# Seven-product units of the feed-forward layers: weight blocks of 256 features, and two up units of each convolved layer as seven products

## Chip, core and metric

The kernel runs on one core of one Trainium2 chip. The metric is the device time of one execution in microseconds, taken as the median of the executions shown. Lower is better.

## What is computed

Two transformer blocks act on one sequence of 512 tokens of 1024 features, in float32. Each of three layers ends in a feed-forward layer; those three are what the change is about (cut from the reference):

```python
gu = n2 @ w_ffn_in[l]                                    # first block, 1024 -> 2 x 2816
ff = (jax.nn.silu(gu[..., :D_FF]) * gu[..., D_FF:]) @ w_ffn_out[l]
...
u = h @ w_up                                             # second block, twice
for j in range(FFN_CONV):
    y = y + u_pad[:, j:j + S, :] * conv_w[j]             # 3 taps over the tokens, and a bias
gate, up = jnp.split(y, 2, axis=-1)
return (jax.nn.silu(gate) * up) @ w_down
```

The first block's layer is called layer 1 here; the second block has two, with a convolution over the tokens after the up projection: layers 2 and 3. The rest (pooling, stick-breaking attention, cross attention, a gated recurrence and latent attention) is not touched.

## The kernel before, in words

Every float32 product is made of three matmuls. `split` (L62 on ScalarE, ACT; L65 on VectorE, DVE) turns a float32 operand into two parts, `hi` (a rounded copy, by ACT) and `lo` (the remainder, source minus `hi`, by DVE). `mm3` then issues hi·hi, hi·lo and lo·hi into one PSUM bank (L108, L109, L110). Weights come by DMA on the SP queue into `raw` tiles and are split into tiles of tag `w`, a ring of 8, which is room for the parts of four blocks. A part can be written only when TensorE (PE) has done with the block four places earlier.

`out_proj`, `ffn` and the helpers are a plain program; a scheduler then fixes the order of the instructions on each engine, and each engine works its own list off in that order, waiting at the head of the list where it must.

`ffn` works through the 2816 = 22 x 128 gate features and as many up features. For f = 0 the program comes from the layer before (`projA_first`). After that the loop takes 256 gate and 256 up features at a time, f = 2, 4, ... 20. There are two ways to make such a piece:

- `projA`, the straight way: 2 feature blocks x 8 rows of 128 inputs x 3 matmuls over all 512 tokens, 48 matmuls of 512 columns. Its weights are two `raw` loads, each split as one 128x1024 tile.
- `seven`: the weights are cut in a 2 x 2 grid (feature block i, input half j), the tokens in two halves, and seven products of sums take the place of eight. A product is here 4 x 3 = 12 matmuls of 256 columns. The sums of weights (`usum`, tiles `u` and `raw`) are made by DVE, the sums of the input once in `x_sums` (tiles `xc`). Three PSUM accumulators X, Y, Z hold the results; ACT copies Y out, and DVE adds the copies to X and Z.

In layer 1 both gate and up pieces go by `seven` (`gate7`, `up7`), interleaved: `tail` carries the last products of an up unit into the next gate unit. In layers 2 and 3 gate pieces go by `seven`, up pieces by `projA`. There `mixed` follows: one ACT instruction and two DVE instructions (L68, tile `y`) for each 128 features, then `Silu` on ACT or a multiplication into `FT` on DVE. Since DVE's list is in order, a part that stands behind an instruction that waits is late with it.

In layer 1 the loop also draws `rotation`, a chain of some 45 small DVE instructions for the sine tables of the last attention.

Of the kernel before, what the change touches and what calls it, by code (L numbers as in the profile page):

```python
# [10 lines left out]
F32 = mybir.dt.float32  # L11
# [23 lines left out]
def kernel(ctx: ExitStack, tc: tile.TileContext, a: dict, out: bass.AP):  # L35
# [13 lines left out]
    sp = ctx.enter_context(pool("sp", bufs=6))  # L49
# [254 lines left out]
    def seven(w, col, ops, xp, dst, c21, done):  # L304

        A = []
        for i in range(2):
            raw = (wp, xp)[i].tile([P, KD, P], F32, tag="raw", name=nm("raw"), bufs=2)  # L310
            load(raw, w[:, col + i * P : col + (i + 1) * P].rearrange("(k p) n -> p k n", p=P))
            A.append([raw.rearrange("p (c j) n -> p j c n", j=2)[:, j] for j in range(2)])
        bY, bXZ = bank("Y"), bank("XZ")
        pY, pX, pZ = bY[:, :256], bXZ[:, :256], bXZ[:, 256:]
# [9 lines left out]
        def usum(a_, b_, o=None):  # L324
            if o is None:
                o = xp.tile([P, 4, P], F32, tag="u", name=nm("u"), bufs=2)
            tt(o, a_, b_, ALU.add)
            return o

        product(pY, A[0][0], (0, 0), True)  # L330
        act(dst[0][:, lf], pY, AF.Copy)
        yield 1
        u1 = usum(A[1][0], A[1][1])
        product(pX, u1, "nT1", True)
        u3 = usum(A[0][0], A[1][0], A[1][0])
# [70 lines left out]
    negC_f = row("negC_f")[:, :P]  # L406
    load(negC_f, a["c_neg_causal"])
    identR = cp.tile([P, P], F32R, name="identR")
    act(identR, ident, AF.Copy)
    negS = cp.tile([P, P], F32R, name="negS")  # L410
    act(negS, negS_f, AF.Copy)
    negC = cp.tile([P, P], F32R, name="negC")
    act(negC, negC_f, AF.Copy)
# [139 lines left out]
    def rotation(E):  # L553

        pos_i = E.tile([P, NT], I32, name="pos_i")
        load(pos_i, a["positions_2"][0].rearrange("(t p) -> p t", p=P))
        pos = E.tile([P, NT], F32, name="pos")
        nc.vector.tensor_copy(pos, pos_i)
        frq = E.tile([P, 32], F32, name="frq")
        load(frq, a["c_freq"].unsqueeze(0).to_broadcast([P, 32]))  # L560

        ang, part, tmp = (E.tile([P, NT, 32], F32, name=nm("rot")) for _ in range(3))
        prod, turn, frac = ang, sinT, cosT
        tt(ang, pos.unsqueeze(2).to_broadcast([P, NT, 32]), frq.unsqueeze(1).to_broadcast([P, NT, 32]), ALU.mult)
# [23 lines left out]
        for n_, c in enumerate(pieces):  # L588
            add_turns(angh.bitcast(F32), c, n_ == 0)
# [189 lines left out]
    def out_proj(w, Y, nk, gpost, gnext, half0, nxt, plain=lambda: None, parts=None):  # L779
# [74 lines left out]
        else:  # L854
# [633 lines left out]
```

## Time and profile before

| | us |
|---|---|
| median of 3 runs | 2029.02 (2028.67 to 2031.72) |
| the profiled execution | 2036.45, its span 2034.6 |
| PE busy / DVE busy / ACT busy | 1990.5 / 1277.1 / 958.0 |
| layer 1, first unit to first matmul of the down projection | 198.0 |
| layer 2, the same with the idle time ahead of it | 211.9 |
| layer 3, the same | 213.1 |

PE is the engine that is busy nearly all the time, so the time is read from PE: how many matmuls it issues, at which spacing, and where it waits. A matmul's own duration is longer than the spacing, because matmuls overlap; the spacing is the difference of two starts. The same is true of DVE: two instructions in a row start closer than the duration of one. The granted TensorE clock is 0.993 of full speed over the span.

### The profile page before, as it was taken

To read this page: it belongs to the slowest core of one execution; us is meant where nothing else is said; L and a number is where in the kernel's file an instruction comes from. 1 tells how busy PE (TensorE), PEld (TensorE's weight loads), DVE (VectorE), ACT (ScalarE), POOL (GpSimd) and SP (SyncE) were. 2 spreads that over 40 slices of the span, in tenths; PEclk is the share of its full clock that TensorE was granted. 3 is DMA by queue.
4 is the path that set the end of the run, shared out by engine and by line. 5 is a ranking of instruction groups with operands and counts; after the bars stand their busy time and mean duration, and the time that the engine had idled before them with its cause. 6 is when DMAs were issued, how large, how long until landed. Compare 5 with 4: busy or idle time off the path is not lost.

```text
span 2034.6 us, 29719 instructions
## 1 busy us (share of the span) xinstructions
PE 1990.5 (98%) x11665; PEld 1701.7 (84%) x11665; DVE 1277.1 (63%) x2293; ACT 958.0 (47%) x1862; POOL 56.4 (3%) x84
## 2 busy tenths in 40 slices
PE   8999999999999999999999999999989999999999
PEld 6877778889999888888888888888887778888887
DVE  5664543489888336666556887853555558887632
ACT  5543452365555227333244555542357545555521
POOL 0000000000000000000010000000021000000000
PEclk9999999999999999999999999999989999999999
DMA  6332224324333332222213233332230113333322
GB/s 223 90 92 73 69 77 124 104 84 125 102 106 105 93 93 84 73 63 72 70 46 89 83 113 96 93 105 93 66 96 32 42 48 106 96 104 94 104 93 83
DMA packets 192482, 183.44 MB, mean 90 GB/s; under 512 B 6999, under 2 KB 159830, under 8 KB 192342
## 3 DMA queue, kind: packets, MB, share of 16 engines
q1 hardware_dynamic: 192342, 181.54, 29.6%
q8 instruction: 92, 1.51, 0.3%
q14 instruction: 48, 0.39, 0.1%
HBM read 179.42 MB, written 2.10 MB: 89 GB/s over the span
## 4 chain that ended last, share of the span: by engine, by line
PE 80%; DVE 9%; DMA 5%; ACT 3%; issue 2%; POOL 1%; SPq 0%; DVEq 0%; POOLq 0%; ACTq 0%
PE B L108 10%; PE B L110 10%; PE B L109 10%; PE A L108 9%; PE A L109 9%; PE A L110 8%; PE hs L1099 2%; DVE wu L65 2%; PE Y L108 2%; PE Y L109 2%; PE Y L110 2%; DMA raw<-in_w_ffn_in_dram 2%; PE XZ L108 2%; PE XZ L109 2%; PE XZ L110 2%
## 5 line engine op out<-in xcount | busy, mean ns | idle before, releaser
L65 DVE TENSOR_TENSOR wlo<-raw,whi 128x1024 fp32r<-128x1024 f32 (+2 forms) x217 | 257.2, 1187 | 343.7 <-ACT whi L62 343.3
L62 ACT ACTIVATE whi<-raw 128x1024 fp32r<-128x1024 f32 (+2 forms) x217 | 223.9, 1033 | 376.5 <-PE B L109 256.5
L108 PE MATMUL A<-XH,whi 128*128 128x512 f32 (+1 forms) x912 | 337.1, 370 | 0.2 <-ACT XH L62 0.2
L109 PE MATMUL A<-XL,whi 128*128 128x512 f32 (+1 forms) x912 | 332.4, 365 | 0.8 <-DVE XL L65 0.8
L110 PE MATMUL A<-XH,wlo 128*128 128x512 f32 (+1 forms) x912 | 331.7, 364 | 0.0
L110 PE MATMUL B<-whi,yc 128*128 128x512 f32 x528 | 208.0, 395 | 0.0
L108 PE MATMUL B<-whi,yc 128*128 128x512 f32 x528 | 207.6, 393 | 0.0
L109 PE MATMUL B<-wlo,yc 128*128 128x512 f32 x528 | 207.3, 393 | 0.0
L110 PEld LDWEIGHTS A<-XH,wlo 128*128 128x128 f32 x912 | 173.1, 190 | 29.5 <-issue 0.2
L109 PEld LDWEIGHTS A<-XL,whi 128*128 128x128 f32 x912 | 173.3, 190 | 26.4 <-DVE XL L65 1.2
L108 PEld LDWEIGHTS A<-XH,whi 128*128 128x128 f32 x912 | 172.8, 190 | 26.8 <-ACT XH L62 0.7
L108 PE MATMUL B<-whi,XH 128*128 128x512 f32 (+2 forms) x416 | 166.8, 402 | 1.3 <-ACT whi L62 1.3
L109 PE MATMUL B<-wlo,XH 128*128 128x512 f32 (+2 forms) x416 | 158.7, 382 | 1.0 <-DVE wlo L65 1.0
L110 PE MATMUL B<-whi,XL 128*128 128x512 f32 (+2 forms) x416 | 158.7, 383 | 0.0
L108 PE MATMUL Y<-xc,wu 128*128 128x256 f32 x480 | 133.8, 279 | 5.0 <-ACT g L62 3.2
L110 PE MATMUL Y<-xc,wu 128*128 128x256 f32 x480 | 133.0, 277 | 0.0
L109 PE MATMUL Y<-xc,wu 128*128 128x256 f32 x480 | 132.9, 277 | 0.0
L62 ACT ACTIVATE wu<-raw 128x512 fp32r<-128x512 f32 x160 | 98.8, 624 | 46.2 <-DMA raw<-in_ffn_w_up_dram 34.9
L62 ACT ACTIVATE wu<-u 128x512 fp32r<-128x512 f32 x120 | 74.4, 629 | 96.8 <-PE A L109 59.8
L109 PEld LDWEIGHTS B<-wlo,yc 128*128 128x128 f32 x528 | 99.3, 188 | 22.7
L110 PEld LDWEIGHTS B<-whi,yc 128*128 128x128 f32 x528 | 99.4, 188 | 21.8
L108 PEld LDWEIGHTS B<-whi,yc 128*128 128x128 f32 x528 | 99.4, 188 | 21.8 <-issue 0.4
(325 smaller groups left out, 4201.0 us busy)
## 6 DMA issues: line engine op xcount, KB each, us to landing
raw<-in_ffn_w_up_dram SPq DMA_DIRECT2D x88, 512.0 KB
raw<-in_w_ffn_in_dram SPq DMA_DIRECT2D x44, 512.0 KB
raw<-in_ffn_w_down_dram SPq DMA_DIRECT2D x44, 512.0 KB
raw<-in_w_in_dram SPq DMA_DIRECT2D x42, 512.0 KB
raw<-in_hgrn_w_in_dram SPq DMA_DIRECT2D x32, 512.0 KB
raw<-in_w_ffn_out_dram SPq DMA_DIRECT2D x22, 512.0 KB
raw<-in_w_out_dram SPq DMA_DIRECT2D x8, 512.0 KB
raw<-in_hgrn_w_out_dram SPq DMA_DIRECT2D x8, 512.0 KB
```

The source lines that it names most:

```text
L62: return nc.scalar.activation(out=out_, in_=in_, func=func, **kw)
L65: return nc.vector.tensor_tensor(out=out_, in0=in0, in1=in1, op=op)
L108: nc.tensor.matmul(out_, lhsT=sta[0], rhs=mov[0], start=first, stop=False, **kw)
L109: nc.tensor.matmul(out_, lhsT=sta[0], rhs=mov[1], start=False, stop=False, **kw)
L110: nc.tensor.matmul(out_, lhsT=sta[1], rhs=mov[0], start=False, stop=last, **kw)
L1099: nc.tensor.matmul(b[:, sl], lhsT=K[:, e, sl], rhs=Q[:, e, sl], start=True, stop=True)
```

## The change

- `seven` now takes blocks of 256 features: a unit covers 512 gate or up features, a product is 24 matmuls of 256 columns into a whole bank (two feature blocks q side by side), a sum or a part is one 128x1024 tile. The weights of a unit are four loads of 128x4x256 in place of two of 128x8x128. The first, (0, 0), goes into the `raw` tiles of the ring pool, the other three into three `raw` tiles of the layer's own pool, which gate and up units share one after the other. There is one `u` tile. Y alternates between the banks c0 and c1, Z between c2 and c3, X is one of the four common banks.
- the loop takes f = 2, 6, 10, 14, 18. In layer 1 all five up units go by `seven` as before; in layers 2 and 3 those of f = 6 and 10 do now, the others stay two `projA`. The new up units keep partial results in `FT` rows 18 to 21.
- `rotation` is drawn by the down projection of layer 1, in one scratch tile; `negC` is loaded ahead of the latent attention; the small tiles' pool `sp` has 5 buffers in place of 6.

```diff
-    def seven(w, col, ops, xp, dst, c21, done):
+    def seven(w, col, ops, xp, place, quarter):
...
+        for i, j in ((0, 0), (1, 0), (1, 1), (0, 1)):
+            if (i, j) == (0, 0):
+                t_ = wp.tile([P, 4, 256], F32, tag="raw", name=nm("raw"), bufs=2)
+            else:
+                t_ = xp.tile([P, 4, 256], F32, tag="raw", name=nm("raw"), bufs=3)
+            src = w[:, col + i * 256 : col + (i + 1) * 256].rearrange("(c j p) n -> p j c n", j=2, p=P)[:, j]
+            load(t_, src)
+            blk[i, j] = t_
+        n_ = uz[0] = uz[0] + 1
+        bY, bX, bZ = bank("Y", f"c{n_ % 2}"), bank("X"), bank("Z", f"c{2 + n_ % 2}")
...
         def product(o, src, key, first):
-            t_ = wp.tile([P, 2, 4, P], F32R, tag="w", name=nm("wu"))
-            split(src, t_[:, 0], t_[:, 1])
+            hi = wp.tile([P, 4, 256], F32R, tag="w", name=nm("wuh"))
+            lo = wp.tile([P, 4, 256], F32R, tag="w", name=nm("wul"))
+            split(src, hi, lo)
             x_ = ops[key]
-            for c in range(4):
-                mm3(o, (t_[:, 0, c], t_[:, 1, c]), (x_[0][:, c], x_[1][:, c]), first and c == 0, c == 3, skip_group_check=True)
+            for q in range(2):
+                f_ = slice(q * P, (q + 1) * P)
+                for c in range(4):
+                    mm3(
+                        o[:, q], (hi[:, c, f_], lo[:, c, f_]), (x_[0][:, c], x_[1][:, c]),
+                        first and q == 0 and c == 0, q == 1 and c == 3, skip_group_check=True,
+                    )
...
+        product(pY, blk[0, 0], (0, 0), True)
+        a_ = kept(pY, 0, 0)
         yield 1
+        u1 = usum(blk[1, 0], blk[1, 1], xp.tile([P, 4, 256], F32, tag="u", name=nm("u")))
         product(pX, u1, "nT1", True)
+        u3 = usum(blk[0, 0], blk[1, 0], blk[1, 0])
+        u2 = usum(u3, blk[1, 1], u1)
         product(pY, u2, "nT2", False)
+        b_ = kept(pY, 0, 1)
+        product(pZ, blk[0, 1], (1, 0), True)
+        quarter(0, 0, pZ, 1.0, a_)
         product(pY, u3, "T3", False)
+        c_ = kept(pY, 1, 1)
+        quarter(1, 1, pX, -1.0, c_)
         yield 1
+        product(pY, blk[1, 1], "T4", False)
+        quarter(1, 0, pY, -1.0, None)
+        product(pX, usum(u2, blk[0, 1], u2), (1, 1), False)
+        quarter(0, 1, pX, 1.0, b_)
...
-            for f in range(0, 22, 2):
-                next(rot, 0)
...
+            for f in range(2, 22, 4):
                 g7 = gate7(f)
                 next(g7)
                 run(tail)
                 next(g7)
-                if conv is None:
+                tail = iter(())
+                if f in ups:
                     tail = up7(f)
                     next(tail)
                     run(g7)
...
                     run(g7)
                     run(u8)
+                    run(projA(w_up, DFF + (f + 2) * P, X, sink(up, f + 2)))
             run(tail)
-            r = out_proj(w_down, FT, 22, gpost(), gnext(), lambda g0: xpool, nxt, parts=E)
+            rot = rotation(E) if conv is None else iter(())
+            r = out_proj(w_down, FT, 22, gpost(), gnext(), lambda g0: xpool, nxt, parts=E, beside=rot)
```

**How the order moves.** In the rows below `wuh` and `wul` are the parts hi and lo of a product's weights, `u` a sum of weights, `raw` a loaded block or a sum made in its place, `X`, `Y`, `Z` the accumulators, `y` the convolution's tile. The numbers tell one tile from another.

DVE in layer 2 with the change, from the sixth product's part of the gate unit of f = 6 to the first sums of the up unit of f = 6:

```order
L65 TENSOR_TENSOR wul_1737_10728<-raw_1711_10531,wuh_1736_10727 128x1024 [waits PE_49,Activation_49]
L65 TENSOR_TENSOR FT_1575_9600<-Z_1715_10537,FT_1575_9600 128x2x256 [waits PE_49]
L65 TENSOR_TENSOR wul_1741_10768<-u_1718_10567,wuh_1740_10767 128x1024 [waits Activation_49]
L65 TENSOR_TENSOR u_1744_10806<-raw_1728_10689,raw_1729_10691 128x1024 [waits DMAHW7_49,DMAHW0_49,DVE_49]
L65 TENSOR_TENSOR raw_1728_10689<-raw_1727_10687,raw_1728_10689 128x1024 [waits DVE_49]
```

and the loads of that up unit on the SP queue:

```order
L77 DMA raw_1728_10689<-in_ffn_w_up_2_dram 128x4x256 [waits DMAHW2_49,DMAHW7_49,DVE_49,Activation_49]
L77 DMA raw_1729_10691<-in_ffn_w_up_2_dram 128x4x256 [waits DVE_49]
L77 DMA raw_1730_10693<-in_ffn_w_up_2_dram 128x4x256 [waits DMAHW1_49,DVE_49]
```

`raw_1729` takes the place of `raw_1711`, so its load waits for the first DVE row above; the fourth row waits for that load. Two instructions stand between. Before, a unit's second block had one of two tiles, and the loads of one unit did not wait for the unit just before it.

DVE in layer 2 with the change, from the gate unit's last drain of f = 10 into the up unit of f = 10:

```order
L68 SCALAR_TENSOR_TENSOR y_1790_11234<-FT_1575_9600,convc_334,y_1790_11234 128x510 [waits DVE_49]
L68 SCALAR_TENSOR_TENSOR y_1791_11239<-FT_1575_9600,convc_334,y_1791_11239 128x510 [waits DVE_49]
L65 TENSOR_TENSOR FT_1575_9600<-X_1758_10935,FT_1575_9600 128x2x256 [waits PE_49]
L65 TENSOR_TENSOR wul_1798_11287<-u_1796_11284,wuh_1797_11286 128x1024 [waits Activation_49]
L68 SCALAR_TENSOR_TENSOR y_1794_11274<-FT_1575_9600,convc_334,y_1794_11274 128x511 [waits Activation_49]
L68 SCALAR_TENSOR_TENSOR y_1795_11279<-FT_1575_9600,convc_334,y_1795_11279 128x511 [waits Activation_49]
L68 SCALAR_TENSOR_TENSOR y_1794_11274<-FT_1575_9600,convc_334,y_1794_11274 128x510 [waits DVE_49]
L68 SCALAR_TENSOR_TENSOR y_1795_11279<-FT_1575_9600,convc_334,y_1795_11279 128x510 [waits DVE_49]
L65 TENSOR_TENSOR u_1796_11284<-raw_1780_11167,raw_1781_11169 128x1024
L65 TENSOR_TENSOR wul_1800_11317<-u_1796_11284,wuh_1799_11316 128x1024 [waits Activation_49]
L65 TENSOR_TENSOR wul_1802_11346<-raw_1782_11171,wuh_1801_11345 128x1024 [waits DMAHW1_49,Activation_49]
L65 TENSOR_TENSOR wul_1804_11375<-raw_1780_11167,wuh_1803_11374 128x1024 [waits Activation_49]
```

DVE at that place before, where the up piece is a `projA`:

```order
L65 TENSOR_TENSOR wlo_1837_11389<-raw_1835_11386,whi_1836_11388 128x1024 [waits DMAHW5_49,PE_49]
L68 SCALAR_TENSOR_TENSOR y_1819_11286<-A_1807_11177,convc_338,y_1819_11286 128x511 [waits Activation_49]
L65 TENSOR_TENSOR wu_1838_11416<-raw_1823_11295,wu_1838_11416 128x512 [waits PE_49,Activation_49]
L68 SCALAR_TENSOR_TENSOR y_1819_11286<-A_1807_11177,convc_338,y_1819_11286 128x510 [waits DVE_49]
L65 TENSOR_TENSOR wu_1840_11438<-u_1829_11333,wu_1840_11438 128x512 [waits PE_49,Activation_49]
L65 TENSOR_TENSOR FT_1624_9915<-FT_1624_9915,y_1819_11286 128x512 [waits DVE_49]
L65 TENSOR_TENSOR wlo_1844_11462<-raw_1842_11459,whi_1843_11461 128x1024 [waits DMAHW6_49,PE_49,Activation_49]
L65 TENSOR_TENSOR g7_1820_11291<-XZ_1825_11298,g7_1820_11291 128x256 [waits PE_49]
```

With the change the parts of the up unit's second and third products (`wul_1798`, `wul_1800`) stand behind the gate unit's last drain of X and behind four and eight `y` instructions; before, the parts of the gate unit's products 6 and 7 (`wu`) and of the straight piece (`wlo`) stood between single `y` instructions.

PE at that place with the change, where the gate unit's last product ends and the up unit's second begins:

```order
L108 MATMUL X_1758_10935<-XH_1576_9601,wuh_1792_11245 128x256
L109 MATMUL X_1758_10935<-XL_1577_9602,wuh_1792_11245 128x256
L110 MATMUL X_1758_10935<-XH_1576_9601,wul_1793_11246 128x256
L108 MATMUL X_1784_11174<-xc_1651_10009,wuh_1797_11286 128x256 [waits Activation_49]
L109 MATMUL X_1784_11174<-xc_1652_10010,wuh_1797_11286 128x256
L110 MATMUL X_1784_11174<-xc_1651_10009,wul_1798_11287 128x256 [waits DVE_49]
```

The product that needs `wul_1798` follows at once on the one whose accumulator DVE drains in the row ahead of `wul_1798`; before, a straight piece of 24 matmuls of 512 columns stood there.

## Rows read from the trace of the kernel before

**Rows 1.** The page: span, and busy time of each engine.

```profile
span 2034.6 us, 29719 instructions
...
PE 1990.5 (98%) x11665; PEld 1701.7 (84%) x11665; DVE 1277.1 (63%) x2293; ACT 958.0 (47%) x1862; POOL 56.4 (3%) x84
```

**Rows 2.** Busy time by stretch: layer 1, its down projection, layer 2, one of its periods, layer 3.

```profile
core 0: us, PE busy (x) PEld busy (x) DVE busy (x) ACT busy (x) POOL busy (x), PEclk, DMA share, GB/s
453.49:651.47 197.98, 192.14 (x1659) 189.80 (x1657) 175.95 (x336) 115.45 (x233) 0.00 (x0) 1.00 0.36 105
651.47:772.00 120.53, 120.21 (x538) 98.81 (x537) 44.28 (x51) 37.52 (x51) 2.20 (x4) 1.00 0.30 92
1126.63:1338.48 211.85, 208.39 (x1323) 186.02 (x1321) 179.49 (x269) 121.79 (x199) 0.00 (x0) 1.00 0.35 102
1226.56:1268.00 41.44, 41.44 (x266) 37.11 (x264) 34.49 (x52) 23.07 (x39) 0.00 (x0) 1.00 0.36 103
1696.28:1909.34 213.06, 209.35 (x1323) 187.38 (x1321) 179.21 (x268) 123.86 (x199) 0.00 (x0) 0.99 0.34 102
```

**Rows 3.** Timeline of PE in layer 2: start, duration, instruction. Two products, then half a straight piece.

```profile
1185.12 0.28 PE L108 MATMUL Y<-xc,wu 128*128 128x256 f32 x1
...
1187.73 0.28 PE L110 MATMUL XZ<-XH,wu 128*128 128x256 f32 x1
1187.84 0.39 PE L108 MATMUL A<-XH,whi 128*128 128x512 f32 x1
...
1193.20 0.40 PE L110 MATMUL A<-XH,wlo 128*128 128x512 f32 x1
1193.44 0.28 PE L108 MATMUL Y<-XH,wu 128*128 128x256 f32 x1
```

**Rows 4.** Timeline of PE in layer 1; in brackets the idle time ahead and what ended it.

```profile
453.49 0.28 PE L108 MATMUL Y<-XH,wu 128*128 128x256 f32 x1
...
524.77 0.39 PE L108 MATMUL XZ<-XH,wu 128*128 128x256 f32 x1 [1.91 <-DVE FT L68]
...
535.30 0.38 PE L108 MATMUL XZ<-XH,wu 128*128 128x256 f32 x1 [0.71 <-DVE u L68]
...
634.40 0.39 PE L108 MATMUL XZ<-XH,wu 128*128 128x256 f32 x1 [0.33 <-DVE u L68]
...
651.47 0.40 PE L108 MATMUL B<-whi,yc 128*128 128x512 f32 x1
```

**Rows 5.** Timeline of PE at the starts and ends of layers 2 and 3.

```profile
1126.51 0.28 PE L110 MATMUL A<-XH,wlo 128*128 128x256 f32 x1
1129.01 0.36 PE L108 MATMUL Y<-XH,wu 128*128 128x256 f32 x1 [2.22 <-DVE y L68]
...
1132.72 0.38 PE L108 MATMUL Y<-xc,wu 128*128 128x256 f32 x1 [0.64 <-ACT g L62]
...
1338.48 0.39 PE L108 MATMUL B<-whi,yc 128*128 128x512 f32 x1
...
1698.14 0.36 PE L108 MATMUL Y<-XH,wu 128*128 128x256 f32 x1 [1.70 <-DVE y L68]
...
1703.12 0.38 PE L108 MATMUL Y<-xc,wu 128*128 128x256 f32 x1 [2.01 <-ACT g L62]
...
1909.34 0.39 PE L108 MATMUL B<-whi,yc 128*128 128x512 f32 x1
```

**Rows 6.** Timeline of DVE at the start of layer 2; xN are N in a row.

```profile
1126.81 2.71 DVE L68 SCALAR_TENSOR_TENSOR y<-A,convc,y 128x511 f32<-128x511 f32 x4
1129.44 1.28 DVE L65 TENSOR_TENSOR wu<-u,wu 128x512 fp32r<-128x512 f32 x2
...
1134.48 1.28 DVE L65 TENSOR_TENSOR FT<-FT,y 128x512 f32<-128x512 f32 x2
1135.68 1.22 DVE L65 TENSOR_TENSOR wlo<-raw,whi 128x1024 fp32r<-128x1024 f32 x1
1136.81 0.68 DVE L65 TENSOR_TENSOR wu<-raw,wu 128x512 fp32r<-128x512 f32 x1
1137.41 0.42 DVE L65 TENSOR_TENSOR g<-XZ,g 128x256 f32<-128x256 f32 x1
1137.75 0.68 DVE L65 TENSOR_TENSOR u<-u,raw 128x512 f32<-128x512 f32 x1
```

**Rows 7.** Groups by line and shape: count, busy us, mean ns, idle time ahead.

```profile
L62 ACT ACTIVATE whi<-raw 128x1024 fp32r<-128x1024 f32 x200 | 211.9, 1061 | 362.3 <-PE B L109 254.3 <-PE A L109 77.2 <-PE XZ L110 6.4
```

**Rows 8.** Timeline of layer 1: a load on the SP queue, and DVE's sum that waits for it.

```profile
526.91 0.37 SPq L77 DMA_DIRECT2D raw<-in_w_ffn_in_dram  x1
...
530.88 0.69 DVE L65 TENSOR_TENSOR u<-raw 128x512 f32<-128x512 f32 x1 [1.66 <-DMA raw<-in_w_ffn_in_dram]
```

More of the change, by code (lines that the diff above doesn't have):

```diff
@@ L48 @@
     gp = ctx.enter_context(pool("gp", bufs=2))
-    sp = ctx.enter_context(pool("sp", bufs=6))
+    sp = ctx.enter_context(pool("sp", bufs=5))
     yp = ctx.enter_context(pool("yp", bufs=6))
@@ L302, in x_sums @@
         return ops
-    def seven(w, col, ops, xp, dst, c21, done):
[L308 to L314, printed above, removed]
-        lf, rt = slice(0, 256), slice(256, 512)
+    uz = [0]
@@ L405 @@
     load(negS_f, a["c_neg_strict"])
-    negC_f = row("negC_f")[:, :P]
-    load(negC_f, a["c_neg_causal"])
     identR = cp.tile([P, P], F32R, name="identR")
     act(identR, ident, AF.Copy)
-    negS = cp.tile([P, P], F32R, name="negS")
+    negS = cp.tile([P, P], F32R, tag="neg", name="negS")
     act(negS, negS_f, AF.Copy)
-    negC = cp.tile([P, P], F32R, name="negC")
-    act(negC, negC_f, AF.Copy)
     def copies(dst, n=S):
@@ L866, in out_proj @@
             for c in range(nch - 2):
+                next(beside, 0)
                 yc = pair_of(c)
@@ L1005, in ffn, with quarter @@
-            rot = rotation(E) if conv is None else iter(())
-            tail = iter(())
-            for f in range(0, 22, 2):
-                next(rot, 0)
-                if f == 0:
-                    sinks[:] = sink(gate, 0), sink(up, 0)
-                    run(steps)
-                    continue
+                left = [2, 2]
+                def quarter(i, l, b, sign, part):
+                    o = at(f, i, l)
+                    if part is None:
+                        act(o, b, AF.Silu if conv is None else AF.Copy, scale=sign)
+                    else:
+                        if sign > 0:
+                            tt(o, b, part, ALU.add)
+                        else:
+                            stt(o, b, sign, part, ALU.mult, ALU.subtract)
+                        if conv is None:
+                            act(o, o, AF.Silu)
+                    left[i] -= 1
+                    if conv is not None and not left[i]:
+                        for q in range(2):
+                            gate(f, 2 * i + q, FT[:, f + 2 * i + q])
@@ L1013, in ffn @@
+            tail = iter(())
+            sinks[:] = sink(gate, 0), sink(up, 0)
+            run(steps)
+            for f in range(2, 22, 4):
                 g7 = gate7(f)
@@ L1037 @@
         lambda X_, pend: projA_first(w_h, (D, 0), X_, (lambda b: sinks[0](b), lambda b: sinks[1](b)), pend),
-        "right",
+        "right", range(2, 22, 4),
     )
@@ L1228 @@
     L, close_L = open_pool("ml")
+    negC_f = row("negC_f")[:, :P]
+    load(negC_f, a["c_neg_causal"])
+    negC = cp.tile([P, P], F32R, tag="neg", name="negC")
+    act(negC, negC_f, AF.Copy)
     g_c = gp.tile([P, 512], F32, tag="g", name=nm("g"))
```

104 lines of the change are left out of this document (47 added, 57 removed).

## The prediction

> **What bounds the kernel now.** I read the page's busy times first: PE works 98% of the span, so the end moves only by the matmuls PE no longer issues, and by the waits it loses or gains. DVE, at 63% over the whole [rows 1], looks far from a bound. The table of stretches, read next, says otherwise: in layers 1 to 3 DVE is busy for 84 to 89% of the stretch, and in one period of layer 2 for 34.5 of 41.4 us; ACT has room everywhere, and the granted clock there is 0.99 to 1.00 [rows 2]. Third, PE's timeline gives prices: a product is 24 matmuls of 256 columns, 2 x 12, in 2.72 us of two in a row, and 24 matmuls of 512 take 5.60 [rows 3]. Last, the waits in brackets: layer 1 is interrupted by short ones that DVE ends [rows 4], layers 2 and 3 wait near their start [rows 5] and hardly at all behind it.
>
> **Matmuls saved.** A straight 512-feature up unit is 4 x 24 matmuls of 512 columns, 4 x 5.60 = 22.40 us; by seven products it is 7 x 24 of 256, 7 x 2.72 = 19.04 [rows 3]. Two units in each of two layers: 4 x 3.36 = **-13.4 us**. Layer 1's units and all gate units keep their number of matmuls, since a unit of 512 replaces two of 256. The spacing in these rows, 233 ns for 512 columns and 113 for 256, stands a little further apart than proportional, which favours small matmuls. The Trainium skill ("TensorE: Matmul & The Clock Gate", section Back-to-back issue gap) gives the isolated gap as 518 and 262 cycles at 2.4 GHz, a fixed part that speaks against narrow matmuls: by it my estimate of the saving is (96 x 518 - 168 x 262) / 2400 = 2.4 us for a unit, 9.5 in all, and the sum below would be 4 higher. The measured spacing decides here.
>
> **Layer 1.** Its 197.98 us [rows 2] hold all but the last two of 140 small products: 138 x 1.36 = 187.7 us. So some 10.3 us are waits, of the kind of [rows 4]. Afterwards a product is twice as long against the same delays, and the small instructions of the rotation, some 45, leave this stretch for the down projection, where DVE is busy for only 44.3 of 120.5 us [rows 2]; that is the cover of the move, and it costs nothing there. DVE's need for a gate and an up unit is 22 parts and sums x 1.13 us, and some 6 us of drains, 31 us, against 14 x 2.72 = 38.1 of PE. What could replace the waits is the `raw` tile that three units share: the sixth product's part must be made (ACT 1.06 [rows 7], DVE 1.13 [rows 6]) before the next unit's load starts; issue to sum is 3.97 [rows 8], then come the sum and another part and two instructions between, about 10.5 us in all; PE has five products, 13.6 us, for it. I take 2 us of remaining waits: **-8.3 us**; bounds -10.3 (no wait left) and 0 (just as many).
>
> **Starts of layers 2 and 3.** A layer's length less ten periods of half of 41.44 [rows 2] is 211.9 - 207.2 = 4.7 and 213.1 - 207.2 = 5.9 us; the waits are 2.22 + 0.64 and 1.70 + 2.01 of it [rows 5]. Y and Z get banks of their own, so the first product no longer waits for the `y` instructions of the accumulator ahead. But the parts are twice as long, and the third product's stands behind thirteen sums and parts and eight `y` [rows 6]; I put some 5 us of stall for each, **-0.5 us** together, bounds -6 and +4.
>
> **The new need of DVE at f = 6 and 10.** This is the large term. With both pieces by seven, DVE has for each pair 22 parts and sums x 1.13 = 24.9 us, 6 drains, 16 `y` x 0.66 = 10.6 and 4 multiplications x 0.60 = 2.4 [rows 6]. A drain of 128x2x256 has no row; two of 256 columns (0.34 each) and one SBUF addition of 512 (0.60) bound it at 0.60 and 0.68 [rows 6], and I take 0.63: 3.8 us. Together 41.7 us, where PE needs 14 x 2.72 = 38.1. **DVE becomes the bound**, where before it had 7 us to spare in a period [rows 2].
>
> How far it falls behind I count along DVE's own list in layer 2, from the first `y` of the straight piece of f = 2 to the part of the straight piece of f = 14. There stand 49 parts and sums x 1.13, 36 `y` x 0.66, 10 multiplications x 0.60 and 13 drains x 0.63: 55.4 + 23.8 + 6.0 + 8.2 = 93.4 us. It starts about 0.8 us after PE's first product of f = 6, behind an ACT instruction of half the width of [rows 7] (an estimate, between half and the whole of its 1.06), so 94.2. PE passes 28 products and five of the next gate unit in that stretch: 33 x 2.72 = 89.8. With DVE never idle PE would lose 94.2 - 89.8, about 4.5 us.
>
> DVE will be idle, though. A second block's load can be issued only behind the sixth part of the unit before; two DVE instructions, about 1.7 us, stand between it and the sum that needs it, against 3.97 of load [rows 8]. That leaves 2.3; where more or less stands between, I read 2.8, 0 and 1.3 from the list: 6.4 us in four units. And in five places a sum is followed by nothing but its own part, so DVE waits for ACT's rounded copy (1.06, [rows 7]) and a little: 1.2 each, 6.0. PE uses hi twice before lo, 0.2 or 0.3 us to the good. A layer then loses 94.2 + 6.4 + 6.0 - 89.8 - 0.3, about 16.5; I take 17, since part of DVE's work before the stretch also slips, **+34 us** for layers 2 and 3. Bounds: 4.5 (all idle time covered) and 21 (the loads take as long again), so +9 to +42.
>
> **Other edits.** The sp pool's five buffers, `negC`'s load and the common scratch tile concern work for which PE's list waits nowhere in the rows: nothing each. If the cover of the down projection failed, the price would be the rotation's few us at most.
>
> **Sum.** -13.4 - 8.3 - 0.5 + 34 = +11.8. The profiled execution took 2036.45, 7.4 above the median of 2029.02; the differences come from its rows and are set against the median: 2029.0 + 11.8, about **2041 us**. A measurement of this kernel can tell about 0.2%, 4 us, from no change.
>
> **Rivals.**
> 1. *The idle time of DVE is absorbed.* ACT makes hi parts ahead, loads are issued early enough, and only the lack of work capacity remains: 4.5 us a layer. -22.2 + 9 = -13.2, **2016 us** (2012 to 2024). For it: before, DVE had 7 us of idle time a period and PE lost nothing [rows 2]. Against: the single `u` tile and the three `raw` tiles forbid making sums early. It decides below 9 us a layer. Chance 0.26.
> 2. *Half absorbed.* 9 to 13 us a layer gives -4 to +4; at 10, -2: **2027 us**. Chance 0.12.
> 3. *Slower for another reason: layer 1's waits stay.* The chain part, load, sum and part of 10.5 us grows beyond 13.6 if the load takes 7 us in place of 3.97 [rows 8], since every unit passes through it. The gain of 8.3 is then gone, and with the main term the time is -13.4 - 0.5 + 34 = +20, **2049 us**. For it: layer 1's waits on loads exist [rows 8]. Against: 3 us to spare. Chance 0.06.
>
> **How the numbers follow.** The main case, 13 to 21 us lost in each of layers 2 and 3, has 0.56: -22.2 + 26 to -22.2 + 42, so 2033 to 2049, its likeliest 2041. With rival 3, slower has 0.62; rival 2 is the same, 0.12; rival 1 faster, 0.26. The range reaches from 2016, the middle of rival 1, to 2050: what lies outside is the lower half of rival 1 (0.13) and the worse half of rival 3.
>
> **What would show it.** Right: the spacing of the new up products is 2.72 us per 24 matmuls; layer 1 shrinks from 198 to about 190 us; from the first unit's start to the first matmul of the down projection layers 2 and 3 grow from 212 and 213 to about 222 us (-6.7 of matmuls, +17 of stalls); between f = 6 and f = 14 PE shows waits of 1 to 4 us ended by DVE's `wul`, most at the second and third products of the up units, with DVE busy for over 85% there and waiting for loads at `u` and for ACT at `wul`. Wrong: PE without waits in that stretch, or layers 2 and 3 at 210 us or less (rival 1); layer 1 still at 198 with waits for `raw` (rival 3); products at another spacing than 2.72, in which case the term of the matmuls is at fault.

## The result, and the profile after

With the change the kernel takes 2046.25 us (median of 4 runs, 2043.25 to 2046.61), against 2028.85 before (4 runs, 2027.88 to 2031.72): ratio 1.0079, 95% interval 1.0059 to 1.0098. It is slower by 17.4 us, where 11.8 were forecast. Among the executions of the experiments below two of the kernel with no up unit by seven ran in a slow state (3479.22 and 5041.6 us) and are left out.

The page's head, as in [rows 1]:

```profile
span 2044.8 us, 29711 instructions
...
PE 1993.9 (98%) x11953; PEld 1718.5 (84%) x11953; DVE 1294.1 (63%) x2043; ACT 948.5 (46%) x1670; POOL 55.4 (3%) x84
```

Busy time by stretch, as in [rows 2]: layer 1, its down projection, layer 2 from the last matmul of the layer before, layer 3 likewise:

```profile
core 0: us, PE busy (x) PEld busy (x) DVE busy (x) ACT busy (x) POOL busy (x), PEclk, DMA share, GB/s
454.60:643.87 189.27, 189.19 (x1635) 188.97 (x1633) 159.24 (x158) 100.67 (x120) 0.00 (x0) 1.00 0.33 101
643.87:766.82 122.95, 122.95 (x563) 101.59 (x562) 55.92 (x97) 39.76 (x55) 2.20 (x4) 1.00 0.28 94
1123.47:1345.39 221.92, 210.98 (x1468) 195.26 (x1467) 191.58 (x221) 124.13 (x158) 0.00 (x0) 0.98 0.29 93
1699.64:1919.99 220.35, 210.48 (x1467) 194.49 (x1466) 191.53 (x221) 125.21 (x159) 0.00 (x0) 0.98 0.30 94
```

Layer 1 is 8.7 us shorter, and PE is idle there for 0.1 us in place of 5.8 (stretch less PE's busy time). Of the 8.7, 2.4 come back in the next stretch, which holds the layer's last products, now twice as long. Layers 2 and 3 are 10.1 and 7.3 us longer. So the three layers with their ends give 11.1 of the loss.

The spans differ by 10.2 us. The profiled execution of before lay 7.4 above its median, that of after 0.4, which gives 10.2 + 7.4 - 0.4 = 17.2. The layers' 11 us leave 6 of that, and in this pair of executions the rest of the span shows none of it (10.2 less 11.1). Part of the 7.4 explains that: between layers 2 and 3 the execution of before takes 357.80 us (1338.48 to 1696.28, granted clock 0.98). The run under "Layer 1 and the rotation" below has the same instructions there and takes 352.61 (1338.48 to 1691.09, clock 1.00). Set against that trace (span 2028.1) the change costs 16.7 us, 13.7 in the layers with their ends and 3.0 outside them.

PE's timeline between f = 6 and f = 14 of layer 2, its four longest waits:

```profile
1221.48 0.39 PE L110 MATMUL Z<-XH,wul 128*128 128x256 f32 x1 [0.66 <-DVE wul L65]
1228.21 0.39 PE L110 MATMUL Y<-XH,wul 128*128 128x256 f32 x1 [0.90 <-DVE wul L65]
1240.82 0.39 PE L110 MATMUL X<-xc,wul 128*128 128x256 f32 x1 [3.33 <-DVE wul L65]
1245.69 0.39 PE L108 MATMUL Y<-xc,wuh 128*128 128x256 f32 x1 [0.68 <-ACT wuh L62]
```

All end with a weights' part, hi or lo. The long one is the up unit's second product at f = 10, the place that the order listings of f = 10 above show. DVE's timeline around it:

```profile
1232.65 1.22 DVE L65 TENSOR_TENSOR wul<-u,wuh 128x1024 fp32r<-128x1024 f32 x1 [1.63 <-ACT wuh L62]
1233.91 1.22 DVE L65 TENSOR_TENSOR u<-raw,raw 128x1024 f32<-128x1024 f32 x1
1235.16 1.23 DVE L65 TENSOR_TENSOR raw<-raw,raw 128x1024 f32<-128x1024 f32 x1
1236.31 2.73 DVE L68 SCALAR_TENSOR_TENSOR y<-FT,convc,y 128x511 f32<-128x511 f32 x4
1238.95 0.68 DVE L65 TENSOR_TENSOR FT<-X,FT 128x512 f32<-128x512 f32 x1
1239.55 1.21 DVE L65 TENSOR_TENSOR wul<-u,wuh 128x1024 fp32r<-128x1024 f32 x1
1240.69 2.73 DVE L68 SCALAR_TENSOR_TENSOR y<-FT,convc,y 128x511 f32<-128x511 f32 x4
1243.33 1.22 DVE L65 TENSOR_TENSOR u<-raw,raw 128x1024 f32<-128x1024 f32 x1
1245.67 1.23 DVE L65 TENSOR_TENSOR wul<-u,wuh 128x1024 fp32r<-128x1024 f32 x1 [1.12 <-ACT wuh L62]
...
1255.01 1.23 DVE L65 TENSOR_TENSOR u<-raw,raw 128x1024 f32<-128x1024 f32 x1 [0.40 <-DMA raw<-in_ffn_w_up_dram]
```

From 1232.65 to 1244.55 DVE works without a gap while PE waits for it. The drain of 128x2x256 takes 0.60 from its start to the next (1238.95 to 1239.55), the `y` 0.66. Where DVE does pause between f = 6 and f = 14, it waits for ACT's copy, but for two places: once for PE's Z, 0.52 us, and once for a load, 0.40.

The same two layers as stretches, from the first product of f = 6 to the first straight matmul of f = 14, and three short pieces of layer 2:

```profile
1173.09:1275.11 102.02, 95.35 (x794) 93.73 (x793) 93.29 (x106) 59.23 (x76) 0.00 (x0) 0.98 0.31 97
1747.29:1849.60 102.31, 95.51 (x793) 93.88 (x792) 92.47 (x106) 58.93 (x75) 0.00 (x0) 0.98 0.30 93
...
1133.62:1139.74 6.12, 5.96 (x26) 5.67 (x27) 5.75 (x5) 2.79 (x3) 0.00 (x0) 0.51 0.25 74
1220.43:1236.99 16.56, 14.72 (x122) 14.01 (x120) 14.86 (x18) 9.01 (x12) 0.00 (x0) 1.00 0.31 96
1240.82:1245.69 4.87, 4.19 (x22) 3.89 (x22) 3.75 (x6) 2.74 (x5) 0.00 (x0) 0.65 0.00 0
```

DVE is busy for 93.3 of 102.0 us. The last row and the third from last show what had not been forecast: behind a long wait the granted clock is low. After 3.84 us of idle time at the start of layer 2 (row below) it is 0.51, the lower level (1.2 GHz), for 6 us; after the 3.33 us at f = 10 it averages 0.65. Behind the shorter waits between 1220 and 1237 it stays at the upper level (1.00, the row between). In layer 3 it falls at both places too, at f = 10 behind a wait of 3.40 and at the layer's start, where three waits of 0.64, 0.45 and 1.81 us stand close together.

```profile
1133.62 0.58 PE L108 MATMUL Y<-xc,wuh 128*128 128x256 f32 x1 [3.84 <-ACT wuh L62]
```

And the price of a product, as in [rows 3], is no longer one number. PE's timeline, the first matmul of three products in a row:

```profile
1173.09 0.28 PE L108 MATMUL Y<-XH,wuh 128*128 128x256 f32 x1
...
1175.81 0.28 PE L108 MATMUL X<-xc,wuh 128*128 128x256 f32 x1
...
1178.63 0.28 PE L108 MATMUL Y<-xc,wuh 128*128 128x256 f32 x1
```

24 matmuls with `XH` as the moving operand take 2.72 us as before, 24 with `xc` 2.82. Before, both took 2.72 (two of 12, [rows 3]).

### The profile page after: what moved, and what is told of

Its sections match the earlier page's. It is cut to its first block, busy times and chain, and to the rows that moved or that the text cites. A ratio compares the mean times of both kernels' runs of the same rounds, so it can differ in the third digit from the quotient of the medians.

```text
span 2044.8 us, 29711 instructions
## 1 busy us (share of the span) xinstructions
PE 1993.9 (98%) x11953; PEld 1718.5 (84%) x11953; DVE 1294.1 (63%) x2043; ACT 948.5 (46%) x1670; POOL 55.4 (3%) x84
## 4 chain that ended last, share of the span: by engine, by line
PE 78%; DVE 12%; DMA 3%; ACT 3%; issue 2%; POOL 1%; SPq 0%; ACTq 0%; DVEq 0%; POOLq 0%
PE B L110 9%; PE B L109 9%; PE B L108 9%; PE A L108 8%; PE A L110 8%; PE A L109 7%; PE Y L110 3%; PE Y L108 3%; DVE wul L65 3%; PE Y L109 3%; DVE y L68 3%; PE hs L1125 2%; DVE u L65 2%; PE X L108 1%; PE X L109 1%
## 5 line engine op out<-in xcount | busy, mean ns | idle before, releaser
L108 PE MATMUL A<-XH,whi 128*128 128x512 f32 (+1 forms) x784 | 286.7, 367 | 0.2 <-ACT XH L62 0.2
L109 PE MATMUL A<-XL,whi 128*128 128x512 f32 (+1 forms) x784 | 281.7, 360 | 0.8 <-DVE XL L65 0.8
L110 PE MATMUL A<-XH,wlo 128*128 128x512 f32 (+1 forms) x784 | 281.3, 359 | 0.3 <-DVE wlo L65 0.2
L110 PEld LDWEIGHTS A<-XH,wlo 128*128 128x128 f32 x784 | 148.2, 189 | 25.1 <-DVE wlo L65 1.1
L108 PE MATMUL Y<-xc,wuh 128*128 128x256 f32 x576 | 162.6, 282 | 5.6 <-ACT wuh L62 5.0
L109 PEld LDWEIGHTS A<-XL,whi 128*128 128x128 f32 x784 | 148.8, 190 | 22.3 <-DVE XL L65 1.2
L108 PEld LDWEIGHTS A<-XH,whi 128*128 128x128 f32 x784 | 148.0, 189 | 22.1 <-ACT XH L62 0.7
L110 PE MATMUL Y<-xc,wul 128*128 128x256 f32 x576 | 162.0, 281 | 1.8 <-DVE wul L65 1.8
L109 PE MATMUL Y<-xc,wuh 128*128 128x256 f32 x576 | 161.7, 281 | 0.0
L65 DVE TENSOR_TENSOR wul<-raw,wuh 128x1024 fp32r<-128x1024 f32 x96 | 115.9, 1219 | 17.4 <-ACT wuh L62 17.4
L62 ACT ACTIVATE wuh<-raw 128x1024 fp32r<-128x1024 f32 x96 | 100.1, 1055 | 52.2 <-PE Y L109 32.1
```

The costliest lines, as they stand in the source:

```text
L62: return nc.scalar.activation(out=out_, in_=in_, func=func, **kw)
L65: return nc.vector.tensor_tensor(out=out_, in0=in0, in1=in1, op=op)
L108: nc.tensor.matmul(out_, lhsT=sta[0], rhs=mov[0], start=first, stop=False, **kw)
L109: nc.tensor.matmul(out_, lhsT=sta[0], rhs=mov[1], start=False, stop=False, **kw)
L110: nc.tensor.matmul(out_, lhsT=sta[1], rhs=mov[0], start=False, stop=last, **kw)
```

## The experiments

Three questions were open: where the slower spacing comes from, whether the waits between f = 6 and 14 are DVE's amount of work or something else, and what made layer 1 shorter. The first two are answered below, the third is not.

### Where the tiles lie

The built programs give each tile an address in bytes. Weights' parts start at 32 modulo 64 in both kernels. The pools behind `sp` moved when `sp` got 5 buffers, and with them `xc` in layer 2 and `XH` in layers 1 and 3:

```
                        before     after
weights (first)          30496     29984    32 modulo 64 in both
XH, layers 1 and 3      103392    102336    32, then 0
xc, layer 2             103392    102336    32, then 0
XH, layer 2             196576    196576    32 in both
xc, layers 1 and 3      184288    180192    32 in both
```

Two kernels add 32 bytes behind the weights, to the changed kernel and to the one before:

```diff
+    pad = sp.tile([P, 8], F32, tag="pad", name="pad", bufs=1)
+    nc.gpsimd.memset(pad, 0.0)
```

> Theory (place of tiles): in the changed kernel's trace products whose moving operand lies in a tile at an address of 0 modulo 64 (weights at 32 modulo 64) have 117.5 ns between matmuls of 256 columns, the others 114.8; the change's smaller sp pool moved every pool behind it by 1056 bytes, and so from 32 to 0. 32 bytes more behind the weights put all back: some 2300 matmuls x 3 ns and 1100 of 512 columns x 3 ns, about -10 us, 2036. Rival (form of the product): the spacing comes from weights of 256 features or from two halves of a bank, then nothing changes, 2046.

Measured: 2036.56 (12 runs, 2032.65 to 2045.55), ratio to before 1.0041 (1.0025 to 1.0057), where the change alone has 1.0079. Products with `xc` and `XH` now go alike in layer 3's timeline:

```profile
1738.74 0.28 PE L110 MATMUL Y<-XH,wuh 128*128 128x256 f32 x1
...
1741.46 0.28 PE L110 MATMUL X<-xc,wuh 128*128 128x256 f32 x1
...
1744.18 0.28 PE L110 MATMUL Y<-xc,wuh 128*128 128x256 f32 x1
```

> The kernel before with the same 32 bytes, which put its pools at 0 modulo 64 and leave all else. Theory (place of tiles): matmuls of the padded tiles go from 113.8 to about 117.5 ns (256 columns), those of 512 lose 3 ns; about +8 us, 2037. Rival (form of the product): no change, 2029.

Measured: 2037.82 (7 runs, 2034.11 to 2039.66), ratio 1.0039 (1.0024 to 1.0053). 32 bytes that do nothing cost the old kernel 8.5 us and give the new one 9.7. Both came out as the place of the tiles has it. The form of the product, which each of these pairs keeps, is excluded as the cause.

Where the 9.7 lie, in one execution of each kernel, is seen in the stretches of the padded one: layer 1, then to the first unit of layer 2, layer 2, to layer 3, layer 3.

```profile
455.19:641.32 186.13, 185.61 (x1635) 185.19 (x1633) 159.59 (x157) 100.34 (x121) 0.00 (x0) 1.00 0.34 103
...
641.32:1117.66 476.34, 471.49 (x2658) 401.89 (x2657) 281.08 (x609) 189.07 (x374) 17.93 (x28) 1.00 0.26 79
1117.66:1339.13 221.47, 208.41 (x1466) 192.86 (x1465) 192.00 (x222) 124.34 (x159) 0.00 (x0) 0.98 0.30 94
1339.13:1690.86 351.73, 343.53 (x1874) 282.36 (x1872) 182.59 (x411) 172.59 (x452) 28.54 (x36) 0.99 0.22 72
1690.86:1911.37 220.51, 209.88 (x1466) 194.33 (x1465) 191.84 (x222) 125.49 (x160) 0.00 (x0) 0.98 0.30 94
```

The same stretches of the kernel with the change alone are 189.27, 479.72, 221.80, 354.36 and 220.24 us long. Layer 1 gains 3.1, the two stretches between the layers 3.4 and 2.6, layers 2 and 3 nothing: there DVE sets the pace. So 6.0 of it lie where the change has nothing to do. These sizes are those of two executions. Five of the padded kernels below have the same program as this one in layer 1 and between the layers; the six traces take 185.7 to 186.1 us for layer 1 in three and 192.7 to 193.1 in the other three, and 476.3 to 480.7 and 350.7 to 353.4 for the two stretches between the layers. Only the last, against 354.36, leaves the spread. The sum of 9.7 is shown by the medians, its places only in part.

A third kernel puts the same 32 bytes ahead of the weights:

```diff
+    pad = cp.tile([P, 8], F32, name="pad")
```

> The kernel before with 32 bytes ahead of the weights' pool: weights and the pools behind them at 0 modulo 64, those placed from the other end stay at 32. Theory A (weights and moving operand want the same remainder): products with both at 0 can go at 113 ns, those with one at 0 and one at 32 go at 117 or more; the time lies between 2029 and the 2037.8 of the other shift. Theory B (the moving operand must lie at 32): all products with it at 0 go at 117 or more, those with it at 32 at 113, whatever the weights; about 2037.

Measured: 2041.23 (6 runs, 2033.59 to 2041.8), ratio 1.0049 (1.0032 to 1.0065), above what either theory gave, so the time speaks for neither. PE's timeline in layer 2, products of 12 matmuls, is clearer; `xc` and the weights lie at 0 modulo 64, `XH` at 32:

```profile
1239.37 0.28 PE L110 MATMUL XZ<-xc,wu 128*128 128x256 f32 x1
...
1240.74 0.28 PE L110 MATMUL Y<-xc,wu 128*128 128x256 f32 x1
...
1242.10 0.28 PE L110 MATMUL XZ<-XH,wu 128*128 128x256 f32 x1
...
1243.51 0.28 PE L110 MATMUL Y<-xc,wu 128*128 128x256 f32 x1
```

Two products with both operands at 0 go in 1.37 and 1.36 us, the one with `XH` at 32 in 1.41. That speaks for theory A: weights and moving operand want the same remainder. It is not all, though: the same remainder allows the quick pace and does not ensure it. In the gates-only kernel with the pad, below, products with equal remainders go at the slow pace through nearly all of layer 1 (2.82 us from start to start):

```profile
606.96 0.28 PE L110 MATMUL Y<-XH,wuh 128*128 128x256 f32 x1
...
609.78 0.28 PE L110 MATMUL Y<-xc,wuh 128*128 128x256 f32 x1
```

There the pace had changed at a wait of 0.44 us near the start of the layer (460.02), and it then held; in the padded kernel the same wait (461.81) changed nothing. 70 products x 0.11 us are 7.7 us, about half of the spread between runs of one kernel (13 us in the padded one). What picks the pace at a wait stays open.

### The up units and DVE's work

No up unit by seven in layers 2 and 3, without and with the pad:

```diff
-    def ffn(w_up, w_down, X, steps, xpool, conv, gpost, gnext, nxt, side="left", ups=(6, 10)):
+    def ffn(w_up, w_down, X, steps, xpool, conv, gpost, gnext, nxt, side="left", ups=()):
```

> The changed kernel with no up unit of layers 2 and 3 by seven. Theory (DVE is the bound only where gate and up both go by seven): PE's waits between f = 6 and 14, 8.3 us in layer 2 and 8.2 in layer 3, and the low clock after the long one, some 2.4 each, go; 13.4 of matmuls less spacing come back: -21 + 11, about 2036. Rival (shared raw tiles: the waits are for loads of big units as such): the waits stay in gate units, 2046 + 11 = 2057.

Measured: 2037.91 (9 runs, 2035.42 to 2041.55), ratio 1.0045 (1.0032 to 1.0058): 8.3 below the changed kernel, near the 2036 of the first theory and far from 2057. (The waits of the changed kernel that the text above puts at 8.3 and 8.2 us are 6.7 and 6.8 by its two rows: 102.02 less 95.35, 102.31 less 95.51.)

> No up unit of layers 2 and 3 by seven, and the 32 bytes. Theory (the two effects add): 2038.7 less some 9 for the place of the tiles, 2030. From the layers: layer 1 gains 12 with the pad (198.0 to 186.1), the starts of layers 2 and 3 lose some 3 each against the kernel before, 2029 - 12 + 6 = 2023. Rival (place of tiles counts only with the up units): 2039.

Measured: 2030.91 (12 runs, 2024.88 to 2040.66), ratio 1.0003 (0.9986 to 1.0019): the two effects add, roughly: 7.0 us for the pad here, 9.7 above. In its trace PE's waits of 0.2 us or more in layers 2 and 3 are those at their starts alone. The 2023 worked out from the layers was missed; layer 1 takes 193.1 us in this trace, at the slow pace, where 186.1 were put. So without the up units the change is worth nothing that can be measured, once the tiles lie as before.

> Up unit by seven at f = 6 alone, with the 32 bytes. Theory (DVE falls behind over a pair and recovers in the next, straight one, which leaves it 7 us): -3.4 of matmuls and about 2 us of waits in each layer, 3 below the same without up units. Rival (each such unit costs its own waits whatever stands beside it): half of the 10 us that f = 6 and 10 lose together, 5, so 3 above it.

Measured (`ups=(6,)`): 2029.62 (11 runs), ratio 0.9991 (0.9978 to 1.0004). One unit by itself does no harm, against gates alone a difference of 1.3 us that its spread does not settle.

> Up units by seven at f = 6 and 14, a straight pair between them, with the 32 bytes. Theory (the deficit adds up only over neighbours): waits of about 2 us at each, none over 2 us, and the clock stays; 6 below no up units, some 10 below f = 6 and 10 (2036.6). Rival (each costs its own): the same as f = 6 and 10.

Measured (`ups=(6, 14)`): 2024.90 (12 runs), ratio 0.9989 (0.9974 to 1.0003), 11.7 below f = 6 and 10. In this kernel the late products of f = 14 and the gate unit of f = 18 share the rows 18 to 21 of `FT`, so what it computes in those eight blocks of features is not the layer's result; the amount of work is the same.

> Up units by seven at f = 2 and 10, the 32 bytes; a straight pair between. Theory (the deficit adds up only over neighbours): as with f = 6 and 14, some 5 to 10 below f = 6 and 10 (2036.6): 2025 to 2031. Rival (f = 2 stands behind the start of the layer, where DVE is late already, and so the deficits add): 2036 or more.

Measured: 2027.37 (12 runs, 2019.0 to 2032.26), ratio 0.9986 (0.9973 to 0.9999), 9.2 below f = 6 and 10 with the same number of products. Two units with a straight pair between them do no harm, neighbours much. This kernel computes everything, and it is the best of those that do: 0.14% below before, an interval that just leaves out no change. The traces show how little apart units gain: layers 2 and 3 together, each from its first unit to the first matmul of the down projection, take 442.0 us with neighbours, 426.9 with f = 6 and 14, 425.9 with f = 2 and 10, and 428.2 with no up unit by seven. The matmuls saved were to give 13.4. With f = 6 and 14 PE is busy for 7.1 us less than with none (412.9 in place of 420.0), and idle for 5.8 us more.

The amount of DVE work itself was changed in two ways. The first leaves it out:

```diff
-            def mixed(b, m):
+            def mixed(b, m, taps=True):
...
+                if not taps:
+                    return y
...
-                u_ = b if conv is None else mixed(b, 22 + f + q)
+                u_ = b if conv is None else mixed(b, 22 + f + q, f not in ups)
```

> f = 6 and 10 with the 32 bytes; the up units by seven of layers 2 and 3 leave out two of the convolution's three taps (16 DVE instructions of 0.66 us in each layer; the output differs in those features). Theory (DVE's amount of work is the bound there): a pair needs 36.4 us of DVE against 38.1 of PE, so the waits between f = 6 and 14 (8.9 and 7.8 us in the padded kernel) and the low clock behind the longest (2) go nearly all: -15 to -20, 2019. Rival (a sum, ACT's copy and the part in a row, whatever DVE's load): they stay, 2036.

Measured: 2021.49 (6 runs, 2014.99 to 2022.84), ratio 0.9960 (0.9945 to 0.9974): 15.1 below the padded kernel. The stretches from f = 6 to f = 14 in layers 2 and 3, first of the padded kernel, then of this one:

```profile
1166.59:1268.56 101.97, 94.00 (x794) 92.38 (x793) 93.45 (x108) 59.24 (x76) 0.00 (x0) 0.98 0.32 97
1738.74:1840.60 101.86, 95.22 (x793) 93.81 (x792) 92.18 (x105) 58.79 (x75) 0.00 (x0) 0.97 0.30 94
```

```profile
1167.51:1259.42 91.91, 90.34 (x794) 89.95 (x792) 84.23 (x92) 59.06 (x76) 0.00 (x0) 1.00 0.34 104
1727.00:1819.01 92.01, 90.34 (x793) 89.96 (x792) 83.84 (x91) 59.07 (x76) 0.00 (x0) 1.00 0.33 103
```

9.2 and 8.3 us less of DVE's work shorten PE's time by 10.1 and 9.9; 2.2 us over 33 x 2.72 = 89.8 are left, and the clock stays at 1.00. ACT's work is the same in both. (By these rows PE's waits in the padded kernel are 8.0 and 6.6, where the text above has 8.9 and 7.8.) The rival of a fixed delay from sum to part falls: DVE still idles for 7.7 us, and PE hardly waits. But amount and order changed together. With fewer `y` the scheduler also set the parts of the second and third products at f = 10 ahead of the gate unit's `y` and its last drain, behind which they stand in the change; DVE's timeline:

```profile
1224.17 1.22 DVE L65 TENSOR_TENSOR wul<-u,wuh 128x1024 fp32r<-128x1024 f32 x1
...
1227.84 1.23 DVE L65 TENSOR_TENSOR wul<-u,wuh 128x1024 fp32r<-128x1024 f32 x1 [1.19 <-ACT wuh L62]
...
1230.24 2.73 DVE L68 SCALAR_TENSOR_TENSOR y<-FT,convc,y 128x511 f32<-128x511 f32 x4
1232.88 0.68 DVE L65 TENSOR_TENSOR FT<-X,FT 128x512 f32<-128x512 f32 x1
```

The two runs that follow help to tell the two apart.

The second hands work to GpSimd:

```diff
+        def gsum(a_, b_, o):
+            nc.gpsimd.tensor_tensor(out=o, in0=a_, in1=b_, op=ALU.add)
+            return o
...
-        u3 = usum(blk[0, 0], blk[1, 0], blk[1, 0])
-        u2 = usum(u3, blk[1, 1], u1)
+        u2 = usum(u1, blk[0, 0], u1)
+        u3 = gsum(blk[0, 0], blk[1, 0], blk[1, 0])
...
-        product(pX, usum(u2, blk[0, 1], u2), (1, 1), False)
+        product(pX, gsum(u2, blk[0, 1], u2), (1, 1), False)
```

> f = 6 and 10 and the 32 bytes, with two of the four sums of weights of every unit (those for products 5 and 7) made by GpSimd, u2 from u1. Theory (DVE's amount of work is the bound): a pair needs 37.2 us of DVE in place of 41.7, less than PE's 38.1; the waits and the low clock behind them go, -18 to 2019. Rival (the order of DVE's list and ACT's copies make the waits): they stay, 2036. Rival 2 (GpSimd is slow with such sums or slows DVE): waits for its sums, above 2040.

Measured: 2049.56 (4 runs), ratio 1.0099 (1.0085 to 1.0113), 13 slower than the padded kernel: rival 2, in both its forms. GpSimd's timeline, DVE's beside the second of these sums, and the stretch from f = 6 to f = 14 of layer 2:

```profile
1182.11 2.43 POOL L345 TENSOR_TENSOR raw<-raw,raw 128x1024 f32<-128x1024 f32 x1 [10.64 <-DVE u L65]
1189.38 3.32 POOL L345 TENSOR_TENSOR u<-u,raw 128x1024 f32<-128x1024 f32 x1 [4.84 <-DVE wul L65]
```

```profile
1190.36 2.90 DVE L68 SCALAR_TENSOR_TENSOR y<-FT,convc,y 128x511 f32<-128x511 f32 x1
```

```profile
1167.28:1272.35 105.07, 93.66 (x771) 92.66 (x770) 95.84 (x97) 60.25 (x78) 25.43 (x9) 0.95 0.29 91
```

A sum takes 2.4 to 3.3 us there, two or three times DVE's 1.13. DVE is slowed too: beside a GpSimd sum a `y` took up to 2.9 us, where the others took 0.74, and a part up to 3.4 where it otherwise took 1.2. So DVE has fewer instructions in the stretch, 97 in place of 108, and is busy for longer, 95.8 us in place of 93.5; the stretch is longer by 3.1. The run thus did not lighten DVE, and it agrees with DVE's amount of work as the bound.

Last, the same work in another order, the fourth product (a plain block) made second:

```diff
         yield 1
+        product(pZ, blk[0, 1], (1, 0), True)
+        quarter(0, 0, pZ, 1.0, a_)
         u1 = usum(blk[1, 0], blk[1, 1], xp.tile([P, 4, 256], F32, tag="u", name=nm("u")))
...
         b_ = kept(pY, 0, 1)
-        product(pZ, blk[0, 1], (1, 0), True)
-        quarter(0, 0, pZ, 1.0, a_)
         product(pY, u3, "T3", False)
```

> f = 6 and 10 and the 32 bytes, with the fourth product of every unit (a plain block, no sum) made second, so that the first sum is needed a product later. Theory (DVE's amount of work is the bound between f = 6 and 14, its list's order at the starts): the starts of layers 2 and 3 lose up to 2.7 us of wait each and their low clock, the sum of the waits between f = 6 and 14 stays at 4.5 or more in a layer but no single one reaches 3 us: -8 to -14, about 2026. Rival (latency alone): the waits at second and third products go, -20, 2017.

Measured: 2046.90 (5 runs), ratio 1.0091 (1.0075 to 1.0108), 10 slower than the padded kernel, and a miss for both expectations. Behind layer 1's down projection the two profiles differ by 2.4 us only, but the longest wait in layer 2 is now one of 5.6 us:

```profile
1231.89 0.58 PE L112 MATMUL Y<-xc,wul 128*128 128x256 f32 x1 [5.59 <-DVE wul L65]
```

The product that waits is the one of `u2`, third in the change and fourth here. From f = 6 to f = 14 layer 2 takes 101.2 us (1177.81 to 1279.05), with DVE busy for 92.0, in place of 102.0 and 93.5: another order, nearly the same work and the same length. That DVE's total work sets the length of layers 2 and 3 agrees with this; that this order would spread the waits does not. Layer 1 lost most: from its first unit to the first matmul of the down projection 195.6 us in place of 186.1. PE is idle there for 4.1 us in place of 0.5; the rest is a lower clock behind one of its waits (0.50 from 474.3 to 477.7) and slower matmuls, of which the order need not be the cause.

Over these four kernels the stretch from f = 6 to f = 14 of layer 2 is as long as DVE is busy in it and 7.7 to 9.3 us more: 102.0 for 93.5, 91.9 for 84.2, 105.1 for 95.8, 101.2 for 92.0.

### Layer 1 and the rotation

```diff
             for f in range(0, 22, 2):
-                next(rot, 0)
...
-            r = out_proj(w_down, FT, 22, gpost(), gnext(), lambda g0: xpool, nxt, parts=E)
+            r = out_proj(w_down, FT, 22, gpost(), gnext(), lambda g0: xpool, nxt, parts=E, beside=rot)
```

> The kernel before with the rotation drawn by the down projection of layer 1 and nothing else. Theory A (products twice as long removed layer 1's waits): layer 1 keeps most of its 10 us of waits, 2029 to 2025. Theory B (the rotation's small DVE instructions made them): layer 1 falls to about 190 us, 2021.

Measured: 2028.51 (12 runs), ratio 0.9996 (0.9985 to 1.0006): no difference. But the edit did not move the rotation. It moved the calls in the program, and the scheduler still set the rotation's instructions ahead of layer 1 and into it: in this trace they run from 439 to 528 us, in that of before from 428 to 525. One of them on DVE's timeline, and the stretch of layer 1:

```profile
507.26 0.23 DVE L74 TENSOR_SCALAR sinT<-sinT 128x128 f32<-128x128 f32 x1
```

```profile
454.39:653.17 198.78, 195.87 (x1658) 194.56 (x1657) 176.88 (x340) 115.98 (x232) 0.00 (x0) 1.00 0.36 104
```

DVE has 340 instructions there, before 336 [rows 2]. In the changed kernel the rotation does run in the down projection, from 644 to 668 us; there its scratch tile has the tag `u` of the layer's sums, which may be what keeps it behind them. So this run tells neither theory from the other, and what made layer 1 shorter stays open: longer products, the rotation gone, or both. Two numbers bear on it. In the trace of before some 2.6 of PE's 5.8 us of idle time come after the last instruction of the rotation, and can hardly be its doing. And here PE idles for 2.9 us (198.78 less 195.87) with the rotation in place, so the idle time also differs with the order or the execution.

## Why the prediction was right, and where it was not

The sign was right, and so were the place and the cause of what DVE does to layers 2 and 3. Of the 17.4 us, though, only 7.3 are the change without its shift of the tiles (2036.56 less the 2029.29 of before beside it); 9.7 are that shift, which had been put at nothing. That the time still came within 6 us of the forecast is partly luck: the terms of the sum that follow were off in both directions.

**DVE as the bound at f = 6 and 10** was right, by the step it was made from. The count along DVE's list gave 93.4 us; DVE was busy for 93.3 and 92.5. PE lost 12.2 and 12.5 us there (102.02 and 102.31 less 89.8), where 16.5 were worked out and 17 taken. Too large was DVE's idle time: 12.4 forecast, 8.7 measured in layer 2 (102.0 less 93.3). The 6.0 for ACT's copies was near, 7.4 (DVE's waits for `wuh` in that stretch). The 6.4 for loads came to one wait of 0.40; no other sum waited for a load. So by this term alone the case was rival 2's (9 to 13 us a layer), half absorbed, and rival 3's load decided nothing, here or in layer 1. Rival 1 fell: far more than 4.5 us was lost.

**The starts of layers 2 and 3** were too small, "some 5 us of stall for each". From the first unit to f = 6 layer 2 takes 49.5 us (1123.59 to 1173.09) for 7 x 2.72 + 22.40 = 41.4, layer 3 47.5: 8.1 and 6.1 lost. The step named the right wait, 3.84 us at the third product in layer 2, and left out what follows it: with the low clock behind it 26 matmuls take 6.12 us in place of 2.9. The same holds for the wait at f = 10.

**The matmuls** fell by the number forecast, but "7 x 2.72 = 19.04" failed by its spacing, 2.82 for the products of tiles at another remainder. The Trainium skill ("TensorE: Matmul & The Clock Gate", section Back-to-back issue gap) gives 262 cycles as the isolated gap of 256 columns, by which 24 matmuls would take an estimated 2.62 us at 2.4 GHz. Both paces in the trace, 2.72 and 2.82, are slower, so this case does not agree with it.

Layer by layer the errors nearly cancel: forecast +10 for each of layers 2 and 3 (-6.7 + 17 less a little at the start), measured +10.1 and +7.3. **Layer 1** was forecast at about 190 and measured at 189.3, with its waits gone. That nearness too is partly luck. The forecast read 10.3 us of the old 198 as waits, but PE was idle for 5.8 of them; the rest was matmuls slower than 1.36 a product, which runs at more than one pace there. And 2.4 of what the stretch lost went into the next one with the last products, so that layer 1 gained 6.3 in place of 8.3. That longer products and the rotation's move took the waits away was argued; no run separates them. The three layers thus make 11.1 us, where the forecast had 11.8.

**"The sp pool's five buffers ... nothing each"** is the step that failed outright. It looked for waits, and the price came without one: the smaller pool moved the later tiles, which costs 9.7 us by the medians. In the two traces 3.1 of it lie in layer 1 and 6.0 between the layers, in work that the prediction had taken as unchanged; against the second trace of the old code 3.0 us lie outside the layers. So the layers' 11 to 14 us and 3 to 6 outside them make up the 17.4 measured.

## What to carry to other kernels

An engine that is 63% busy over the whole can be the bound of one stage: add its work in list order between two points and set it against the same span of the bounding engine. Spread a stage's extra work between pieces that leave slack; two such units apart were some 9 us cheaper than two neighbours. When a pool changes its size, look at the addresses behind it before explaining a small difference by the edit that was meant. And when an edit moves a piece of program, look in the trace whether its instructions moved.

## What was not expected of the hardware

- The spacing of matmuls depends on where the operands lie: with weights and moving operand at different remainders modulo 64, 24 matmuls of 256 columns took about 2.82 us, with equal ones 2.72 or 2.82. In one trace the second pace set in at a wait of 0.44 us and held for the rest of the layer. 32 bytes moved a kernel of 2029 us by 8.5.
- Waits of 3.3 to 3.8 us were followed by the lower granted clock (averages of 0.65 over 4.9 us and 0.51 over 6.1), and so were three waits of 0.64, 0.45 and 1.81 us close together. Single waits of 0.66 and 0.90 us were not, nor was one of 2.22 in the kernel before.
- GpSimd needed 2.4 to 3.3 us for a 128x1024 sum that takes DVE 1.13, and a DVE instruction of 0.74 us took up to 2.9 beside it.
